# The S5 chunk recurrence: 64 sequential steps over pairs of chunks replaced by a tree with two more levels

## The chip, the core and the metric

The kernel runs on one NeuronCore of a Trainium2 chip, in one launch. The time is device microseconds of that core. Five engines run side by side and meet through semaphores: TensorE (PE, matrix products), VectorE (DVE), ScalarE (ACT), GpSimd (POOL) and SyncE (SP, which issues most of the DMAs).

## What is computed

Two trunk layers for 1024 latent tokens and 128 prompt ("context") tokens, with shared weights. Layer 0 feeds a differential attention and an S5 state-space mixer from one input projection; layer 1 is a pooling mixer; each layer ends in a squared-ReLU MLP. The change concerns the S5 mixer alone, whose core in the reference is

```python
bu = einsum(u, b_bar)                      # per token, 32 groups x 64 complex states, two directions
elems = (broadcast(a), bu)                 # h[t] = a * h[t-1] + bu[t], complex
_, _, h_re, h_im = lax.associative_scan(complex_affine_combine, elems, reverse=reverse, axis=1)
y = einsum(h_re, c_re) - einsum(h_im, c_im)
```

The state `h` at the end of the prompt's scan is an output too.

## The kernel before

**Layout of the scan.** The tokens are cut into chunks of C8 = 8. That leaves NCL = 128 chunks of the latent tokens and NCX = 16 of the prompt. A tile `ST` (128 partitions = two directions x 64 states) holds for real and imaginary part (2), for each of the G = 32 groups, SLOTS = 147 chunk states of 4 bytes each in a row: slots 0 to 128 are the latent's, from CX0 = 130 on the prompt's. Matrix products put each chunk's own contribution there; what is left is the recurrence over chunks, `state[c+1] += a^8 * state[c]`, a complex product and sum.

**The levels.** `carry(..., 1, ...)` first adds, for all pairs of chunks at once, the odd slot into the even one (level 0, on DVE and POOL, while the products land). Then `scan_step(j)`, j = 0 to 63, walks the even slots one after another with a^16 (`ar16`, `ai16`): four DVE instructions (`t1 = cur*ar`, `t2 = swapped cur*ai`, `t1 + t2`, `nxt + t1`), each over 2 x 32 = 64 elements per partition, and in the first eight steps over 128, since the prompt's chain is walked beside the latent's. Last, `carry(..., 2, ...)` fills in the odd slots, for two groups at a time. The two temporaries are the tiles `sc1`, `sc2`; the traces name all of them `sc`.

**Where the steps stand.** After the S5 inputs the kernel runs 36 *blocks*, n = 0 to 35: 12 weight tiles (query, key, value of four heads) times three column blocks of 384 tokens. A block takes 24 matrix products (`pmm`) on PE; DVE multiplies the sum by the row norm (`zz <- pmm,y` or `vz <- pmm,y` in `unscaled`), ACT adds a bias and, for queries and keys, copies the two halves crosswise, DVE multiplies by the cosines (`zz <- zz,cos`), POOL does the sine part, and the result is written out by SP while the next block runs (`finish`). In nearly the same blocks POOL builds 16 output tables of the S5 mixer (`in_ri`, `in_t`, six instructions each, `s5_table`; DVE the first of them), PE makes window products of them (`pk`) and the modulation vectors (`pm`). The scan steps are strewn over these blocks: `scan(SC(n)[0])` behind `zz <- pmm,y`, `scan(SC(n)[1])` after the middle of the block. `SC` gives none for n < 4 and two and two from then on, so 64 steps fill the blocks 4 to 19. The second `carry` follows from block 21 on, the output products from block 24.

**What sets the order.** From block 3 on (`i == 1`) all five engines are pinned to program order (`pinned.update(PIN)`), so each engine's queue runs as the code is written. The pmm sums have four buffers in PSUM, the `zz`/`vz` tiles three.

Of the kernel before, what the change touches and what calls it, by code (L numbers as in the profile page):

```python
# [8 lines left out]
F32 = mybir.dt.float32  # L9
# [3 lines left out]
ALU = mybir.AluOpType  # L13
# [14 lines left out]
G = 32  # L28
C8 = 8
NCL, NCX = TL // C8, TX // C8  # L30
CX0 = NCL + 2
# [6 lines left out]
EPS = 1e-6  # L38
RB = 3
CV = 5  # L40
SC = lambda n: (0, 0) if n < 4 else (2, 2)
PIN = "TPVSA"
PINA = "T"
L0 = (3,)
# [28 lines left out]
def build(nc, tc, a, o, probe=None):  # L73
    pinned = set()

    class Engine:
# [5 lines left out]
        def __getattr__(self, op):  # L82
            f = getattr(self.e, op)

            def call(*args, **kw):
                ins = f(*args, **kw)  # L86
                if self.name in pinned:
# [5 lines left out]
    V, A, T, P, S_ = (Engine(n, e) for n, e in (("V", nc.vector), ("A", nc.scalar), ("T", nc.tensor),  # L93
                                                ("P", nc.gpsimd), ("S", nc.sync)))
# [25 lines left out]
    def tt(e, out, x, y, op):  # L120
        return e.tensor_tensor(out, x, y, op=op)

    def stt(e, out, x, s, y, op0, op1):
        e.scalar_tensor_tensor(out, x, s, y, op0=op0, op1=op1)
# [53 lines left out]
    YB = [3]  # L178
    H = Pool("H", side="left")
    UR = Pool("u", side="left")  # L180
    ar8, ai8, ar16, ai16 = (UR([128, 2, G], F32, nm) for nm in ("ar8", "ai8", "ar16", "ai16"))

    def u_tile():
        return UR([128, C8, UC], F32, "U", bufs=4)
# [295 lines left out]
    pw = S([128, 2, 9, G], F32, "pw")  # L480
# [4 lines left out]
    def cmul(e, ore, oim, xr, xi, yr, yi, tmp, neg_im=False):  # L485
# [11 lines left out]
         b2(0, 2).to_broadcast([128, 2, G]), b2(1, 2).to_broadcast([128, 2, G]), ptmp[:, :2])  # L497
    cmul(V, pw[:, 0, 5:9], pw[:, 1, 5:9], pw[:, 0, 1:5], pw[:, 1, 1:5],
         b2(0, 4).to_broadcast([128, 4, G]), b2(1, 4).to_broadcast([128, 4, G]), ptmp)
    V.tensor_copy(ar8, pw[:, 0, 8:9].to_broadcast([128, 2, G]))  # L500
    V.tensor_scalar(ai8[:, 0], pw[:, 1, 8], -1.0, None, op0=ALU.mult)
    V.tensor_copy(ai8[:, 1], pw[:, 1, 8])
    tt(V, ar16, ar8, ar8, ALU.mult)
    tt(V, ai16, ai8, ai8, ALU.mult)
    tt(V, ar16, ar16, ai16, ALU.subtract)
    stt(V, ai16, ar8, 2.0, ai8, ALU.mult, ALU.mult)

    fden = S([128, 3, G], F32, "fden")
    tt(V, fden[:, 0], lre, lre, ALU.mult)
# [113 lines left out]
    ST = R([128, G, 2, SLOTS], F32, "ST").rearrange("p g r s -> p r g s")  # L623
# [14 lines left out]
    def proj_load(i):  # L638
        if i < 12:
            wq[i] = W([128, KT, 128], F32, "raw1")  # L640
            dma(wq[i], a["w_in"][4 + i])
# [12 lines left out]
    for gi, g0 in enumerate(range(0, G, 3)):  # L654
        n = min(3, G - g0)
# [19 lines left out]
    RP = Pool("rope", side="right")  # L675
# [53 lines left out]
    dma(sin, a["sin"])  # L729
    rp = lambda shape, dt, name: RP(shape, dt, name, bufs=3, tag="rp")  # L730

    def scan_step(j):
        sh = [128, 2, G]
        if j < NCX // 2:
            cur = ST[:, :, :, 2 * j:2 * j + CX0 + 1:CX0]
            nxt = ST[:, :, :, 2 * j + 2:2 * j + CX0 + 3:CX0]
            sh = sh + [2]
            ar, ai = ar16[:, :, :, None].to_broadcast(sh), ai16[:, :, :, None].to_broadcast(sh)
        else:
            cur, nxt, ar, ai = ST[:, :, :, 2 * j], ST[:, :, :, 2 * j + 2], ar16, ai16  # L740
        t1 = RP(sh, F32, "sc1")
        t2 = RP(sh, F32, "sc2")
        tt(V, t1, cur, ar, ALU.mult)
        tt(V, t2, cur[:, ::-1], ai, ALU.mult)
        tt(V, t1, t1, t2, ALU.add)
        tt(V, nxt, nxt, t1, ALU.add)

    pvt = Pool("pvt", side="right", space=PSUM)
    psn.close()
# [20 lines left out]

        finish(last)

    step = [0]

    def scan(n):
        for _ in range(n):
            if step[0] < NCL // 2:
                scan_step(step[0])
                step[0] += 1

    def unscaled(b, p, cf, z):

        tt(V, z, p, ys[b], ALU.mult)
        scan(SC(n)[0])
        for s0, s1, q in SEGS[b]:
            A.activation(z[:, s0:s1], z[:, s0:s1], AF.Identity, bias=cf[:, q:q + 1])

    def qk_block(h, kind, b, p, cf, mid):
# [9 lines left out]
        mid()  # L798
        scan(SC(n)[1])

# [20 lines left out]
    def v_block(h, b, p, cf, mid):  # L821
# [3 lines left out]
        mid()  # L825
        scan(SC(n)[1])

# [15 lines left out]
    def out_tiles(oc):  # L843

        if oc % 2 == 0:
            m = UR([128, BBN], F32, "mE", tag="bb")
            ori = S3([128, 2, 4, 128], F32, "ori", tag="craw")
            return (ori[:, 0], ori[:, 1]), m[:, :512].rearrange("p (g x) -> p g x", g=4), (
                UR([128, 2, 2, UC], F32, "E", tag="pout"), m[:, 512:].rearrange("p (r g c) -> p r g c", r=2, g=2))
        ori = [S3([128, 4, 128], F32, nm, tag="in_ri", bufs=2) for nm in ("orr", "oii")]  # L850
        return ori, S3([128, 4, 128], F32, "mt"), [W([128, 2, 2, UC], F32, "E", tag="raw", bufs=2) for _ in range(2)]

    def out_load(oc, ori, mt):
        g0 = 4 * oc
        for r, x in enumerate(ori):
            dma(x, oS[r, g0:g0 + 4].rearrange("g p m -> p g m"))
        dma(mt, mS[g0:g0 + 4].rearrange("g s h x -> (s h) g x"))
# [79 lines left out]
    def after(n):  # L937
        i, k = divmod(n, 3)
        for m in range(G // 2):
            if tab_at(m) == n:  # L940
                tabs[m] = s5_table(m)
                tabs[m][0]()
        oc = n - NS
        if 0 <= oc < 8:
            assert step[0] >= NCL // 2
            ori, mt, E = outs[oc] = out_tiles(oc)
            out_load(oc, ori, mt)

    def post(n):
        oc = n + 1 - NS  # L950
        if 0 <= oc < 8:
            assert step[0] >= NCL // 2
            for g2 in range(2):
                carry(V, 4 * oc + 2 * g2, 2, 2, *(RP([128, 2, 2, UC // 2], F32, nm) for nm in ("sc1", "sc2")))
        oc = n - NS
        if 0 <= oc < 8:
            for g2 in range(2):
                out_states(oc, g2, outs[oc][2][g2])
# [3 lines left out]
    n, loads = 0, None  # L962
    for i in range(12):
        h, kind = divmod(i, 3)
        if i == 1:
            pinned.update(PIN)
        proj_load(i + 1)
        w, cf = wq.pop(i), None
        for b in (2, 0, 1):
            p, last, *c = project(w, b)  # L970
            cf = c[0] if c else cf
            before(n)
            if n in KN:
                keys_in(KN[n])
            (qk_block if kind < 2 else v_block)(h, *((kind,) if kind < 2 else ()), b, p, cf, lambda: after(n))
            post(n)
            if b == 2:
                proj_split(i + 1)
            if n == NS + 9:
                S3.close()  # L980
                R.close()
                UR.close()
                HB = Pool("heads", side="right")
                KL = [[HB([128, KEYS + TX], F32R, f"Kl{j}{m}") for m in range(2)] for j in range(2)]
                for kl in KL:
                    for m in range(2):
                        P.memset(kl[m].bitcast(F32)[64 - 64 * m:128 - 64 * m], 0.0)
                loads = load_head(0)
            if loads:
                next(loads, None)  # L990
            n += 1
        if kind == 1 and h not in KH:
            keys_in(h)
        if step[0] == NCL // 2:
            step[0] += 1
            sfin = RP([128, 2, G], F32, "sfin")
            V.tensor_copy(sfin, ST[:, :, :, UC])
            dma(o["ns"], sfin)
# [23 lines left out]
    cur = {}  # L1022
# [291 lines left out]
    for b in range(NB):  # L1314
        t = BB([128, KT, BX], F32R, "blk", bufs=3)
        for k in range(4):
            src = hid([128, BN], F32, ("ph", "pl")[k % 2])
# [58 lines left out]
    t0, t1 = MODV[0]  # L1376
# [356 lines left out]
```

## Time and profile before

| | us |
|---|---|
| three runs, median (lowest to highest) | 2555.7 (2552.96 to 2557.45) |
| the profiled execution, its time | 2552.76 |
| its span, first to last instruction | 2551.0 |
| busy: PE / DVE / ACT / POOL | 2399.8 / 1792.0 / 877.2 / 267.0 |
| blocks 4 to 19, by the DVE's `pmm,y` rows | 178.0 to 312.0 |

Read the page by stage. Its line of forty slices (each 63.8 us) has PE at 9 tenths in nearly all of the span, but at 6 to 8 in most of the first eight slices, where DVE stands at 7 to 9. The shares over the whole span hide that; the views that follow are of the stretch 178 to 312 us.

### The profile page before, as it was taken

The page shows a single profiled execution, that of the slowest core. Times are in us where ns is not written, and L with a number is a line of the kernel's source. Part 1 is how long each engine was busy: PE and PEld are TensorE (multiplying, and loading weights), DVE is VectorE, ACT ScalarE, POOL GpSimd, SP SyncE. Part 2 cuts the span into 40 slices and gives each one's busy share as a digit, 9 for nine tenths or more (in the row PEclk, how much of TensorE's full clock was granted, in tenths as well). Part 3 has the DMA queues.
Part 4 walks back from the last instruction along what each step waited for, and adds up shares of the span by engine and source line. Part 5 has one row for each costly group of instructions (what it writes and reads, how often), then busy time and mean ns, then how long its engine had stood idle before and what let it go on. Part 6 is the DMA issues. An engine that isn't in the chain of part 4 may idle for free.

```text
span 2551.0 us, 36404 instructions
## 1 busy us (share of the span) xinstructions
PE 2399.8 (94%) x14070; PEld 2296.1 (90%) x14070; DVE 1792.0 (70%) x3583; ACT 877.2 (34%) x1663; POOL 267.0 (10%) x274
## 2 busy tenths in 40 slices
PE   7987898898997999999999999889999999999996
PEld 3876697787897999999999999879999999999996
DVE  7379865889788777767777655886565555555557
ACT  4453365777615221222222222562122222222214
POOL 5455612100000000000000000120000000000002
PEclk8998998999998999999999999989999999999998
DMA  6334688423353232322332110011111111111102
GB/s 244 82 104 126 192 200 229 105 57 81 129 191 108 67 91 68 98 75 75 91 91 79 50 34 25 1 50 50 42 50 34 50 34 50 34 50 42 42 9 74
DMA packets 106491, 210.86 MB, mean 83 GB/s; under 512 B 10576, under 2 KB 67664, under 8 KB 105936
## 3 DMA queue, kind: packets, MB, share of 16 engines
q1 hardware_dynamic: 104080, 203.01, 27.0%
q10 hardware_dynamic: 2240, 5.54, 0.6%
q8 instruction: 111, 1.82, 0.3%
q14 instruction: 60, 0.49, 0.1%
HBM read 176.95 MB, written 31.56 MB: 82 GB/s over the span
## 4 chain that ended last, share of the span: by engine, by line
PE 64%; DVE 11%; issue 5%; ACT 4%; DMA 4%; POOL 1%; SPq 0%; POOLq 0%; DVEq 0%; ACTq 0%
PE p L86 61%; DVE mj L86 2%; DVE blk L86 1%; DMA raw<-in_w_dram 1%; DVE sc L86 1%; DMA raw<-in_mod_v_dram 1%; PE SP L86 1%; DVE nm L86 1%; ACT e L86 1%; PE tp L86 1%; DVE x L86 1%; DVE s L86 1%; ACT blk L86 1%; DVE zz L86 1%; DVE w2l L86 1%
## 5 line engine op out<-in xcount | busy, mean ns | idle before, releaser
L86 PE MATMUL p<-blk,wh 128*128 128x384 f32 (+1 forms) x3072 | 794.2, 340 | 0.0
L86 DVE SCALAR_TENSOR_TENSOR x<-p,modc,x 128x384 f32<-128x384 f32 (+2 forms) x1056 | 513.6, 513 | 142.6 <-PE p L86 138.7
L86 PEld LDWEIGHTS p<-blk,wh 128*128 128x128 f32 x3072 | 561.5, 189 | 1.6 <-issue 1.2
L86 PE MATMUL p<-blk,wl 128*128 128x384 f32 (+1 forms) x1536 | 520.8, 339 | 0.0
L86 PE MATMUL p<-ph,w2h 128*128 128x384 f32 x1536 | 514.9, 335 | 3.7 <-DVE x L86 3.7
L86 PE MATMUL p<-pl,w2h 128*128 128x384 f32 x1536 | 513.9, 335 | 0.0
L86 PE MATMUL p<-ph,w2l 128*128 128x384 f32 x1536 | 513.6, 334 | 0.0
L86 ACT ACTIVATE r<-r,cf 128x384 f32<-128x384 f32 (+2 forms) x256 | 129.8, 531 | 691.6 <-DVE r L86 691.5
L86 PEld LDWEIGHTS p<-ph,w2h 128*128 128x128 f32 x1536 | 288.3, 188 | 6.2 <-DVE x L86 3.6
L86 PEld LDWEIGHTS p<-blk,wl 128*128 128x128 f32 x1536 | 289.5, 188 | 0.1
L86 PEld LDWEIGHTS p<-pl,w2h 128*128 128x128 f32 x1536 | 288.3, 188 | 0.3
L86 PEld LDWEIGHTS p<-ph,w2l 128*128 128x128 f32 x1536 | 288.3, 188 | 0.1
L86 DVE TENSOR_TENSOR r<-p,y 128x384 f32<-128x384 f32 x192 | 106.2, 554 | 188.9 <-PE p L86 188.7
L86 ACT ACTIVATE wh<-raw 128x1024 fp32r<-128x1024 f32 x80 | 84.7, 1060 | 349.7 <-PE p L86 312.1
L86 DVE SCALAR_TENSOR_TENSOR mj<-raw,cb 128x1024 f32<-128x1024 f32 x128 | 156.1, 1220 | 13.6 <-DMA raw<-in_mod_v_dram 12.6
L86 ACT ACTIVATE w2h<-raw 128x1024 fp32r<-128x1024 f32 x74 | 77.3, 1057 | 221.2 <-PE p L86 161.5
L86 PE MATMUL pmm<-lo,wh 128*128 128x384 f32 (+1 forms) x384 | 137.8, 359 | 7.8 <-DVE lo L86 7.5
L86 PE MATMUL pmm<-hi,wh 128*128 128x384 f32 (+1 forms) x384 | 141.0, 368 | 0.8 <-ACT wh L86 0.8
L86 PE MATMUL pmm<-hi,wl 128*128 128x384 f32 (+1 forms) x384 | 136.6, 356 | 1.2 <-DVE wl L86 1.2
L86 DVE TENSOR_TENSOR s<-r 128x384 f32<-128x384 f32 x192 | 106.5, 555 | 40.1 <-ACT r L86 40.0
L86 POOL TENSOR_TENSOR pl<-pl,mx 128x256 f32<-128x256 f32 x18 | 18.6, 1039 | 1024.1 <-ACT pl L86 1024.1
L86 DVE TENSOR_TENSOR wl<-raw,wh 128x1024 fp32r<-128x1024 f32 x76 | 98.7, 1300 | 22.1 <-ACT wh L86 21.8
(278 smaller groups left out, 3346.5 us busy)
## 6 DMA issues: line engine op xcount, KB each, us to landing
raw<-in_w_dram SPq DMA_DIRECT2D x128, 512.0 KB, 3.6
raw<-in_mod_v_dram SPq DMA_DIRECT2D x64, 512.0 KB, 3.6
raw<-in_mod_w_dram SPq DMA_DIRECT2D x25, 512.0 KB, 4.6
raw<-in_w_in_dram SPq DMA_DIRECT2D x16, 512.0 KB, 4.8
Kd<-kS SPq DMA_DIRECT2D x32, 176.0 KB, 4.8
qS<-zz SPq DMA_DIRECT2D x12, 384.0 KB, 2.7
Q<-qS SPq DMA_DIRECT2D x32, 144.0 KB, 4.7
x<-in_x_dram SPq DMA_DIRECT2D x3, 1536.0 KB, 7.3
```

Source lines behind the costliest of these rows:

```text
L86: ins = f(*args, **kw)
```

## The change

`scan_step` is replaced by a generator `scan_pieces`. Level 0 and its counterpart (`carry`) stay as they are. On the 64 even slots two more levels are put: level 1 joins slots 2 and 4 of each group of four chunks (multiplier a^16, 32 joins per group of states in the latent's row, so every fourth slot is read), level 2 joins slots 4 and 8 of each eight (a^32, 16 joins, every eighth slot). What is left is walked sequentially over every eighth slot with a^64: 16 steps. Then the two levels are walked back down to fill in the slots between. A level is cut into pieces of at most 256 elements: level 1 into eight pieces of four groups each (2 x 4 x 32) and one for the prompt (2 x 32 x 4), level 2 into four of eight groups (2 x 8 x 16) and one for the prompt (2 x 32 x 2). Up and down that is 2 x (9 + 5) = 28 pieces. A piece, as a step, is four DVE instructions. `SC` becomes one call behind `pmm,y` and two after the middle, so the 44 calls fill the blocks 4 to 18 (the last call, the 45th, ends the generator). The multipliers a^8, a^16, a^32 and a^64 are squared from one another in the prologue (four instructions each on 32 or 64 elements) and held without the doubled real part.

```diff
-SC = lambda n: (0, 0) if n < 4 else (2, 2)
+SC = lambda n: (0, 0) if n < 4 else (1, 2)
...
-    ar8, ai8, ar16, ai16 = (UR([128, 2, G], F32, nm) for nm in ("ar8", "ai8", "ar16", "ai16"))
+    pws8 = [(UR([128, 1, G], F32, f"ar{8 << i}"), UR([128, 2, G], F32, f"ai{8 << i}")) for i in range(4)]
...
-    V.tensor_copy(ar8, pw[:, 0, 8:9].to_broadcast([128, 2, G]))
+    ar8, ai8 = pws8[0]
+    V.tensor_copy(ar8[:, 0], pw[:, 0, 8])
     V.tensor_scalar(ai8[:, 0], pw[:, 1, 8], -1.0, None, op0=ALU.mult)
     V.tensor_copy(ai8[:, 1], pw[:, 1, 8])
-    tt(V, ar16, ar8, ar8, ALU.mult)
-    tt(V, ai16, ai8, ai8, ALU.mult)
-    tt(V, ar16, ar16, ai16, ALU.subtract)
-    stt(V, ai16, ar8, 2.0, ai8, ALU.mult, ALU.mult)
+    for (ar, ai), (ar2, ai2) in zip(pws8, pws8[1:]):
+        tt(V, ar2, ar, ar, ALU.mult)
+        tt(V, ai2[:, 0:1], ai[:, 0:1], ai[:, 0:1], ALU.mult)
+        tt(V, ar2, ar2, ai2[:, 0:1], ALU.subtract)
+        stt(V, ai2, ar.to_broadcast([128, 2, G]), 2.0, ai, ALU.mult, ALU.mult)
...
-    def scan_step(j):
-        sh = [128, 2, G]
-        if j < NCX // 2:
-            cur = ST[:, :, :, 2 * j:2 * j + CX0 + 1:CX0]
-            nxt = ST[:, :, :, 2 * j + 2:2 * j + CX0 + 3:CX0]
-            sh = sh + [2]
-            ar, ai = ar16[:, :, :, None].to_broadcast(sh), ai16[:, :, :, None].to_broadcast(sh)
-        else:
-            cur, nxt, ar, ai = ST[:, :, :, 2 * j], ST[:, :, :, 2 * j + 2], ar16, ai16
-        t1 = RP(sh, F32, "sc1")
-        t2 = RP(sh, F32, "sc2")
+    def advance(src, dst, lvl, g0, n, cnt, every):
+
+        cur = ST[:, :, g0:g0 + n, src:src + every * (cnt - 1) + 1:every]
+        nxt = ST[:, :, g0:g0 + n, dst:dst + every * (cnt - 1) + 1:every]
+        ar, ai = (t[:, :, g0:g0 + n, None].to_broadcast([128, 2, n, cnt]) for t in pws8[lvl])
+        t1 = RP([128, 2, n, cnt], F32, "sc1")
+        t2 = RP([128, 2, n, cnt], F32, "sc2")
         tt(V, t1, cur, ar, ALU.mult)
         tt(V, t2, cur[:, ::-1], ai, ALU.mult)
         tt(V, t1, t1, t2, ALU.add)
         tt(V, nxt, nxt, t1, ALU.add)
 
+    def scan_pieces():
+
+
+        def level(lvl, first, second):
+            span = 2 << lvl
+            cnt = NCL // span
+            n = min(G, 128 // cnt)
+            for g0 in range(0, G, n):
+                advance(first, second, lvl, g0, n, cnt, span)
+                yield
+            advance(CX0 + first, CX0 + second, lvl, 0, G, NCX // span, span)
+            yield
+
+        yield from level(1, 2, 4)
+        yield from level(2, 4, 8)
+        for j in range(NCL // 8):
+            if j < NCX // 8:
+                advance(8 * j, 8 * j + 8, 3, 0, G, 2, CX0)
+            else:
+                advance(8 * j, 8 * j + 8, 3, 0, G, 1, 1)
+            yield
+        yield from level(2, 0, 4)
+        yield from level(1, 0, 2)
...
     def scan(n):
         for _ in range(n):
-            if step[0] < NCL // 2:
-                scan_step(step[0])
-                step[0] += 1
+            if not scanned[0] and next(steps, 0) == 0:
+                scanned[0] = 1
```

On DVE, at the start of block 4 (a key block), the rows before are the first two steps and the cosine product behind them:

```order
L86 TENSOR_TENSOR zz<-pmm,y_386 128x384
L86 TENSOR_TENSOR sc_1654<-ST,ar_107 128x128
L86 TENSOR_TENSOR sc_1655<-ST,ai_108 128x128
L86 TENSOR_TENSOR sc_1654<-sc_1654,sc_1655 128x128
L86 TENSOR_TENSOR ST<-ST,sc_1654 128x2x32x2
L86 TENSOR_TENSOR sc_1660<-ST,ar_107 128x128
L86 TENSOR_TENSOR sc_1661<-ST,ai_108 128x128
L86 TENSOR_TENSOR sc_1660<-sc_1660,sc_1661 128x128
L86 TENSOR_TENSOR ST<-ST,sc_1660 128x2x32x2
L86 TENSOR_TENSOR zz<-zz,cos 128x384
```

The same place on DVE now:

```order
L86 TENSOR_TENSOR zz<-pmm,y_398 128x384
L86 TENSOR_TENSOR sc_1666<-ST,ar_107 128x256
L86 TENSOR_TENSOR sc_1667<-ST,ai_108 128x256
L86 TENSOR_TENSOR sc_1666<-sc_1666,sc_1667 128x256
L86 TENSOR_TENSOR ST<-ST,sc_1666 128x2x4x32
L86 TENSOR_TENSOR zz<-zz,cos 128x384
```

One piece of 256 elements stands where two steps of 128 stood; its last index (32) runs over every fourth slot of `ST`, where before the last index (2) ran from the latent's slot to the prompt's.

On DVE in block 10 (a query block, in the middle of the scan), before, from the norm product to the cosine product:

```order
L86 TENSOR_TENSOR zz<-pmm,y_386 128x384
L86 TENSOR_TENSOR sc_2156<-ST,ar_107 128x64
L86 TENSOR_TENSOR sc_2157<-ST,ai_108 128x64
L86 TENSOR_TENSOR sc_2156<-sc_2156,sc_2157 128x64
L86 TENSOR_TENSOR ST<-ST,sc_2156 128x2x32
L86 TENSOR_TENSOR sc_2162<-ST,ar_107 128x64
L86 TENSOR_TENSOR sc_2163<-ST,ai_108 128x64
L86 TENSOR_TENSOR sc_2162<-sc_2162,sc_2163 128x64
L86 TENSOR_TENSOR ST<-ST,sc_2162 128x2x32
L86 TENSOR_TENSOR zz<-zz,cos 128x384
```

And now:

```order
L86 TENSOR_TENSOR zz<-pmm,y_398 128x384
L86 TENSOR_TENSOR sc_2132<-ST,ar_111 128x64
L86 TENSOR_TENSOR sc_2133<-ST,ai_112 128x64
L86 TENSOR_TENSOR sc_2132<-sc_2132,sc_2133 128x64
L86 TENSOR_TENSOR ST<-ST,sc_2132 128x2x32
L86 TENSOR_TENSOR zz<-zz,cos 128x384
```

Here one step of 64 elements, one of the 16 sequential ones, stands between the two products instead of two.

## Rows read from the trace of the kernel before

**Rows 1.** Chain of waits in 258 to 312 us, shares of that stretch by line.

```profile
by line: DVE sc L86 32.1%; DVE zz L86 11.3%; DVE ST L86 8.4%; DMA raw<-in_mod_w_dram 7.7%; DMA vS<-vz 6.7%; issue 5.4%; DMA kS<-zz 5.1%; DVE wl L86 3.1%; PE pk L86 2.3%; SPq L86 2.2%; PE pm L86 1.9%; DVE vz L86 1.0%; DVE chl L86 0.8%; ACT k
```

**Rows 2.** Stretches: from:to, length, busy us (instructions) of each engine, granted clock.

```profile
core 0: us, PE busy (x) PEld busy (x) DVE busy (x) ACT busy (x) POOL busy (x), PEclk, DMA share, GB/s
178.00:220.50 42.50, 31.59 (x230) 28.54 (x229) 39.68 (x93) 11.41 (x27) 25.27 (x34) 0.88 0.44 117
220.50:264.10 43.60, 36.72 (x236) 29.36 (x235) 41.86 (x97) 15.95 (x34) 27.31 (x34) 0.85 0.36 102
264.10:312.00 47.90, 44.09 (x311) 34.79 (x309) 43.23 (x114) 15.69 (x35) 26.91 (x37) 0.99 0.67 198
```

**Rows 3.** The same view of the scan's instructions alone (tile sc, DVE).

```profile
178.00:312.00 134.00, 97.52 (x256) 0.91 0.49 141
```

**Rows 4.** DVE's timeline, an undisturbed 64-element step and the next one's start.

```profile
200.45 0.27 DVE L86 TENSOR_TENSOR sc<-ST,ar 128x64 f32<-128x64 f32 x1
...
200.92 0.23 DVE L86 TENSOR_TENSOR sc<-sc,sc 128x64 f32<-128x64 f32 x1
201.18 0.27 DVE L86 TENSOR_TENSOR ST<-ST,sc 128x64 f32<-128x64 f32 x1
201.49 0.27 DVE L86 TENSOR_TENSOR sc<-ST,ar 128x64 f32<-128x64 f32 x1
```

**Rows 5.** DVE's timeline, an undisturbed 128-element step and the next one's start.

```profile
191.05 0.39 DVE L86 TENSOR_TENSOR sc<-ST,ar 128x128 f32<-128x128 f32 x1
...
191.79 0.29 DVE L86 TENSOR_TENSOR sc<-sc,sc 128x128 f32<-128x128 f32 x1
192.11 0.41 DVE L86 TENSOR_TENSOR ST<-ST,sc 128x128 f32<-128x128 f32 x1
192.56 0.41 DVE L86 TENSOR_TENSOR sc<-ST,ar 128x128 f32<-128x128 f32 x1
```

**Rows 6.** DVE's timeline, an undisturbed `carry` of 292 elements, every second slot.

```profile
327.87 0.47 DVE L86 TENSOR_TENSOR sc<-ST,ar 128x292 f32<-128x292 f32 x1
...
328.74 0.46 DVE L86 TENSOR_TENSOR sc<-sc,sc 128x292 f32<-128x292 f32 x1
329.24 0.46 DVE L86 TENSOR_TENSOR ST<-ST,sc 128x292 f32<-128x292 f32 x1
```

**Rows 7.** DVE groups in 475 to 700 us: form, count, busy us, mean ns.

```profile
L86 DVE SCALAR_TENSOR_TENSOR blk<-uf,blk 128x256 fp32r<-128x256 f32 x3 | 1.9, 643 | 0.0
L86 DVE SCALAR_TENSOR_TENSOR blk<-uf,blk 128x128 fp32r<-128x128 f32 x3 | 1.2, 415 | 0.0
```

**Rows 8.** DVE's timeline, a 64-element step beside POOL's work, and the next step's start.

```profile
208.64 0.52 DVE L86 TENSOR_TENSOR sc<-ST,ar 128x64 f32<-128x64 f32 x1
...
210.65 0.52 DVE L86 TENSOR_TENSOR sc<-ST,ar 128x64 f32<-128x64 f32 x1
```

**Rows 9.** POOL's timeline in the same microseconds.

```profile
208.44 0.65 POOL L86 TENSOR_TENSOR in_t<-pout,craw 128x256 f32<-128x256 f32 x1
209.16 0.72 POOL L86 TENSOR_TENSOR in_ri<-in_ri,in_t 128x256 f32<-128x256 f32 x1
209.84 0.64 POOL L86 TENSOR_TENSOR in_ri<-pout,craw 128x256 f32<-128x256 f32 x1
210.44 0.64 POOL L86 TENSOR_TENSOR in_t<-pout,craw 128x256 f32<-128x256 f32 x1
```

**Rows 10.** DVE's timeline, block 20, which has no steps between its products.

```profile
312.00 0.55 DVE L86 TENSOR_TENSOR zz<-pmm,y 128x384 f32<-128x384 f32 x1
314.31 0.56 DVE L86 TENSOR_TENSOR zz<-zz,cos 128x384 f32<-128x384 f32 x1 [1.77 <-ACT zz L86]
```

**Rows 11.** DVE's timeline in the prologue: the squarings and what follows.

```profile
19.04 0.22 DVE L86 TENSOR_TENSOR ar<-ar,ai 128x64 f32<-128x64 f32 x1
19.17 0.69 DVE L86 TENSOR_TENSOR bb<-ff,in_ri 128x512 f32<-128x512 f32 x1
...
24.81 2.01 DVE L86 TENSOR_TENSOR wl<-raw,wh 128x1024 fp32r<-128x1024 f32 x1
26.75 11.46 DVE L86 SCALAR_TENSOR_TENSOR lo<-x,avec,hi 128x384 fp32r<-128x384 f32 x8
```

**Rows 12.** PE's timeline: its first wait for those.

```profile
28.42 0.44 PE L86 MATMUL pmm<-lo,wh 128*128 128x384 f32 x1 [3.89 <-DVE lo L86]
```

More of the change, by code (lines that the diff above doesn't have):

```diff
@@ L771, in keys_in @@
         finish(last)
-    step = [0]
+    steps, scanned = scan_pieces(), [0]
     def scan(n):
         for _ in range(n):
-            if step[0] < NCL // 2:
-                scan_step(step[0])
-                step[0] += 1
+            if not scanned[0] and next(steps, 0) == 0:
+                scanned[0] = 1
     def unscaled(b, p, cf, z):
@@ L944, in after @@
         if 0 <= oc < 8:
-            assert step[0] >= NCL // 2
+            assert scanned[0]
             ori, mt, E = outs[oc] = out_tiles(oc)
@@ L951, in post @@
         if 0 <= oc < 8:
-            assert step[0] >= NCL // 2
+            assert scanned[0]
             for g2 in range(2):
@@ L993, in build @@
             keys_in(h)
-        if step[0] == NCL // 2:
-            step[0] += 1
+        if scanned[0] == 1:
+            scanned[0] = 2
             sfin = RP([128, 2, G], F32, "sfin")
```

## The prediction

> **What bounds the kernel now.** The page's share of busy time says PE, and for most of the span that is so. The scan does not live there: it lives in blocks 4 to 19, 178 to 312 us, so I read that stretch by itself. First its busy times, in three parts [rows 2]: DVE is busy 39.7 of 42.5, 41.9 of 43.6 and 43.2 of 47.9 us, together 124.8 of 134.0; PE 31.6, 36.7 and 44.1, together 112.4. So DVE is the full engine here, by a wide margin in the first part, by a small one in the second, and level with PE in the third. Then the scan's own share [rows 3]: 256 instructions, 97.5 us, nearly three quarters of the stretch. Then the chain of waits for its last part [rows 1]: the scan's rows (sc and ST) are 40.5% of what released the end, the other rope products of DVE 12%, and the DMAs in it are issued behind a DVE result. So what DVE spends on the scan in this stretch is paid in time, nearly one for one, until PE takes over.
>
> **What a step costs now.** Undisturbed, a 64-element step runs from 200.45 to 201.49, 1.04 us [rows 4], and a 128-element step from 191.05 to 192.56, 1.51 us [rows 5]. 56 of the one and 8 of the other are 58.2 + 12.1 = 70.3 us. The scan really takes more. Its 97.5 us are busy time; after three of the four instructions of a step there is a gap of about 0.03 us (200.92 + 0.23 to 201.18 [rows 4]), 64 x 0.09 = 5.8 us, so it holds DVE for 103.3 us. The other 33.0 us are a meeting with POOL: beside POOL's table work the same step takes from 208.64 to 210.65, 2.01 us [rows 8], while POOL completes three instructions (starts 208.44 to 210.44) [rows 9]. That is 0.97 us more for three, 0.32 us for each POOL instruction. POOL runs 34 + 34 + 37 = 105 instructions in the stretch [rows 2], and 33.0 / 105 is 0.31, so one price for each POOL instruction accounts for all of it.
>
> **What a piece of 256 elements costs.** No row shows that shape, so I bound it. The lower end is the `carry`, which reads every second slot, 8 bytes apart: 292 elements from 327.87 to 329.24 + 0.46 and a gap, 1.86 us [rows 6]; 36 elements fewer, at the 1.0 ns an element that the contiguous sum shows (0.23 to 0.29 us for 64 more [rows 4, 5]), four times, are 0.15 less: 1.71 us. The upper end comes from the 128-element step. There the instructions that touch `ST` grow from 0.27 to 0.41 us for 64 elements more, 2.2 ns an element, twice the contiguous sum's [rows 4, 5]: reading far apart (the two elements of a row are 520 bytes apart) costs double. 128 elements more are then 3 x 0.28 + 0.13 = 0.97 on top of 1.51: 2.48 us. Which end holds for slots 16 bytes apart (level 1) and 32 bytes apart (level 2)? For 32 bytes there is a row: the split of the GELU result writes and reads every eighth element, and it takes 415 ns for 128 elements and 643 for 256, 1.8 ns an element [rows 7]; with that slope a piece is 1.51 + 3 x 0.23 + 0.13 = 2.33. For 16 bytes there is none. I take double cost there too, since every element of a 16-byte stride is as alone as at 32 bytes, and 2.4 us for a piece, between 2.33 and 2.48.
>
> [...]
>
> **The change, term by term.**
> 1. Pieces and steps, undisturbed. A sweep is 9 + 4 pieces at 2.4 and one of 128 elements at 1.51: 32.7 us, two sweeps 65.4. The sequential part is 2 steps at 1.51 and 14 at 1.04: 17.6. Together 83.0 against 70.3: **+12.7 us**. The instructions fall from 256 to 176, but the elements that each of the four goes over in all rise from 56 x 64 + 8 x 128 = 4608 to 26 x 256 + 4 x 128 + 14 x 64 = 8064, most of them at double price.
> 2. The meeting with POOL. The number of POOL instructions is the same, and by the count above the price goes by them: 0. Bounds: if it is paid for each DVE instruction, 33.0 / 256 = 0.129 each and 80 fewer, -10.3; if it grows with the time that the scan holds DVE, 33.0 x 12.7 / 70.3 = +6.0. I take 0, because 64- and 128-element instructions both fit the price for each POOL instruction.
> 3. The cover of ACT's latency. `zz <- zz,cos` can start 2.31 us after `zz <- pmm,y` starts, when ACT is free [rows 10]. Two steps of 1.04 behind 0.48 of the product filled that; one step does not (1.52), and DVE would wait 0.8 us. This concerns blocks 9 to 13 (queries and keys that have one sequential step there); a piece of 2.4 covers it, and so does one step beside POOL (0.48 + 2.01). Between 0 and 5 x 0.8 = 4; I take **+2**. Queued behind that wait on DVE is the rest of the block's scan, and nobody but DVE's own next block waits for it.
> 4. Block 19 has no scan any more. Its old steps are in the 103.3, so that gain is inside term 1.
> 5. The multipliers. Eight more small instructions in the prologue, 0.13 us each from start to start between others (19.04 to 19.17), 0.22 alone [rows 11]: 1.0 to 1.8. DVE has no gap there down to the first `lo`, for which PE waits 3.89 us [rows 12], so it is paid: **+1.2**.
> 6. What PE takes back. In the third part PE is busy 44.1 of 47.9 [rows 2], so a longer DVE there is not paid in full where PE would have been late anyway; and PE may use up to four finished sums as a store. Between 0 and -4; I take **-2**.
>
> The sum is 12.7 + 0 + 2 + 1.2 - 2 = +13.9 us. The profiled execution took 2552.76 us (span 2551.0 and 1.8 around it), so it would become 2566.7. That execution is as fast as the fastest of the three runs; on their median of 2555.7 the sum gives **2569.6 us**, 0.54% slower.
>
> **The rivals.**
> *An instruction is the price, faster.* If a DVE instruction here costs a fixed time, the meeting with POOL included, plus 1.0 ns an element wherever the elements lie, fewer and longer instructions win. The place is the 28 pieces: 26 x (1.71 - 2.4) = -17.9 on term 1 makes it -5.2, and term 2 goes to -10.3. With the 2 of term 3 and 1.2 of term 5: -12.3, 2543.4 us. It decides from the piece's price: the 28 pieces may take 103.3 less the sequential part (17.6 and its share of POOL, about 8), 77.7 us, 2.8 us each with POOL's part; below that the change gains, and my forecast has 65.4 + 25, 3.2 each. For it speaks the `carry` at 1.0 ns an element [rows 6]; against it the doubled slope of 128 elements and of the 32-byte rows [rows 5, 7].
> [...]
> *Half of it, no difference.* Either level 1 reads at full rate (18 x 0.69 = -12.4 on term 1) or the meeting with POOL is paid for each instruction (-10.3), not both: +1.5 to +3.6, about 2558 us. For the first speaks that no row shows 16 bytes; for the second that the 64-element rows beside POOL are stretched one by one.
> *More than the sum, slower.* Longer instructions hold POOL up, POOL holds DVE up in turn for as long as the scan lasts (+6.0), the cover of term 3 fails in full (+2 more) and PE gives nothing back (+2): +24, 2579.5 us. POOL's 79.5 busy us of 134 [rows 2] leave it room, which speaks against it.
> That the change does not do what it says I leave out: the new order shows 176 instructions of the shapes named.
>
> **How the numbers follow.** What this kernel's measurement can tell from no change is about 0.2%, 5 us: 2550.6 to 2560.8. The forecast (2562 to 2575) has a chance of 0.55, the worse case 0.13; both are slower, 0.68. Half of it is 0.17 and counts as the same. The instruction as the price is 0.15, faster. The range leaves out the faster rival and little else: from 2551 (the half case with a little more) to 2581.
>
> **What would show each step.** In the changed kernel's groups, `sc <- ST,ar` of 256 elements at a minimum of 0.65 to 0.70 us says double cost, 0.42 to 0.45 says full rate; level 1 (2x4x32) and level 2 (2x8x16) can be told apart by their place, blocks 4 to 6 and 7. The scan's busy time in its stretch should be some 110 us for 176 instructions; near 90 the faster rival holds. Block 19 should start at about 312 + 6 us or later, though it is the first without scan. A wait of `zz <- zz,cos` for ACT should stand in blocks 9 to 13, up to 0.8 us each. POOL's instructions should number the same and be some tenths longer beside a piece. The prediction is wrong if the 256-element instructions read at full rate, or if the stretch grows and later stages close the gap: PE then would show fewer waits between 312 and 420 us.

## The result, and the profile after

The changed kernel takes 2566.4 us (median of four runs, 2563.5 to 2568.1) against 2554.3 (2552.9 to 2557.5), slower by 12.0 us. The recorded ratio is 1.0053 with a 95% interval of 1.0041 to 1.0065, which would be 13.5 us; beside the later experiments the kernel before had medians of 2552.0 to 2553.2, and against those it is 13.2 to 14.4. So the loss is 12 to 14 us; where a difference to after is taken below, it is taken from 12.0. Forecast were 2569.6 us and slower. The sign and nearly the size are right, but four of the six terms that make up the sum are off by amounts that happen to cancel.

The profiled execution of after took 2566.43 us, its span is 2563.9 (2551.0 before). Three starting points of a block say where the 12.9 us of span lie. Block 4, the first with scan, starts 4.4 us late (182.4 for 178.0). Block 20 starts 16.0 us late (328.0 for 312.0), so blocks 4 to 19 take 145.6 us instead of 134.0, +11.6. At the end 12.9 are left: 3.1 are given back behind the scan.

The same three stretches as [rows 2], by blocks, and the scan's instructions alone as in [rows 3]; the columns are those of before (length; busy us and count of PE, PEld, DVE, ACT, POOL; granted clock; DMA share; GB/s):

```profile
182.40:232.30 49.90, 36.51 (x249) 33.24 (x248) 48.59 (x73) 11.43 (x28) 30.41 (x34) 0.83 0.38 103
232.30:275.00 42.70, 33.61 (x217) 25.90 (x216) 37.02 (x78) 15.96 (x34) 27.62 (x33) 0.83 0.35 101
275.00:328.00 53.00, 46.52 (x299) 36.11 (x298) 48.05 (x73) 15.89 (x35) 28.58 (x32) 0.88 0.63 179
...
182.40:328.00 145.60, 105.49 (x176) 0.85 0.46 130
```

DVE's instructions in the three stretches fall from 304 to 224 and its busy time rises from 124.8 to 133.7 us. The scan's own went from 97.5 us for 256 to 105.5 for 176. The first and the last stretch, where the pieces of 256 elements stand, became longer; the middle one, of single steps, holds DVE for less and still takes 42.7 us, which is a wait, shown further down. The granted clock is lower than before in each (0.83, 0.83 and 0.88 for 0.88, 0.85 and 0.99); PE stands idle for 29.0 us here instead of 21.6, and the chain names DVE.

The chain of waits for the last part (270 to 328 us), in the columns of [rows 1]:

```profile
by line: DVE sc L86 35.9%; DVE ST L86 11.3%; DVE zz L86 10.2%; DMA raw<-in_mod_w_dram 6.9%; DMA kS<-zz 4.7%; issue 4.7%; PE pk L86 3.6%; PE pm L86 3.3%; DVE wl L86 3.0%; ACT zz L86 2.9%; DVE vz L86 1.9%; PE pvt L86 1.5%; DVE chl L86 0.7%; S
```

The scan's share (sc and ST) is 47%, from 40.5%: DVE sets the end of this stretch still, and a little more so.

DVE's timeline of after, an undisturbed piece on the way down (level 1, every fourth slot) with the start of the next (start, duration):

```profile
297.52 0.60 DVE L86 TENSOR_TENSOR sc<-ST,ar 128x256 f32<-128x256 f32 x1
298.03 0.61 DVE L86 TENSOR_TENSOR sc<-ST,ai 128x256 f32<-128x256 f32 x1
298.68 0.42 DVE L86 TENSOR_TENSOR sc<-sc,sc 128x256 f32<-128x256 f32 x1
299.14 0.61 DVE L86 TENSOR_TENSOR ST<-ST,sc 128x256 f32<-128x256 f32 x1
299.78 0.60 DVE L86 TENSOR_TENSOR sc<-ST,ar 128x256 f32<-128x256 f32 x1
```

A piece takes 2.26 us. The three instructions that touch `ST` take 0.60 or 0.61 each, the sum of the two temporaries, which lie in a row, 0.42. A level-2 piece, every eighth slot, shows the same duration in block 7:

```profile
216.34 0.60 DVE L86 TENSOR_TENSOR sc<-ST,ar 128x256 f32<-128x256 f32 x1
```

So slots 16 and 32 bytes apart cost the same (0.60), and both cost more than the 292 elements at 8 bytes of [rows 6] (0.47).

The waits of the cosine product, first all of them in 182.4 to 328.0, from the groups of DVE (count; busy us, mean ns; idle before):

```profile
L86 DVE TENSOR_TENSOR zz<-zz,cos 128x384 f32<-128x384 f32 x10 | 7.6, 756 | 6.2 <-ACT zz L86 6.2
```

and then the one in block 12, in DVE's timeline:

```profile
256.62 0.55 DVE L86 TENSOR_TENSOR zz<-pmm,y 128x384 f32<-128x384 f32 x1
257.09 0.28 DVE L86 TENSOR_TENSOR sc<-ST,ar 128x64 f32<-128x64 f32 x1
...
257.83 0.27 DVE L86 TENSOR_TENSOR ST<-ST,sc 128x64 f32<-128x64 f32 x1
259.12 0.56 DVE L86 TENSOR_TENSOR zz<-zz,cos 128x384 f32<-128x384 f32 x1 [1.02 <-ACT zz L86]
```

One step stands between the two products, and DVE then idles 1.02 us until ACT has written `zz`. In blocks 9 to 13 these waits are 0.56, 0.82, 0.86, 1.02 and 1.12 us, 4.4 together, and 1.77 more in block 19, which has no scan any more.

The prologue, on DVE (the last two instructions of the new squarings, between other work):

```profile
24.54 1.08 DVE L86 TENSOR_TENSOR ar<-ar,ai 128x32 f32<-128x32 f32 x1
25.65 1.27 DVE L86 COPY pout<-pw 64x512 f32<-64x512 f32 x1
26.96 2.18 DVE L86 TENSOR_TENSOR wl<-raw,wh 128x1024 fp32r<-128x1024 f32 x1
29.06 1.12 DVE L86 SCALAR_TENSOR_TENSOR ai<-ar,ai 128x64 f32<-128x64 f32 x1
30.11 1.47 DVE L86 SCALAR_TENSOR_TENSOR lo<-x,avec,hi 128x384 fp32r<-128x384 f32 x1
```

on POOL, beside them,

```profile
24.29 1.28 POOL L86 TENSOR_TENSOR in_t<-pin,bb 128x512 f32<-128x512 f32 x1
...
28.02 2.09 POOL L86 TENSOR_TENSOR in_ri<-pin,bb 128x512 f32<-128x512 f32 x1
```

and on PE, whose wait for `lo` answers to [rows 12]:

```profile
31.63 0.69 PE L86 MATMUL pmm<-lo,wh 128*128 128x384 f32 x1 [7.09 <-DVE lo L86]
```

These two instructions, of 32 and 64 elements, took 1.08 and 1.12 us while POOL worked on 512 elements. The first `lo` is 3.4 us later than in [rows 11] and PE's wait 3.2 us longer.

### The profile page after: what moved, and what is told of

The parts are those of the page before. It is cut to its first block, busy times and chain, and to the rows that moved or that the text cites. A ratio compares the mean times of both kernels' runs of the same rounds, so it can differ in the third digit from the quotient of the medians.

```text
span 2563.9 us, 36332 instructions
## 1 busy us (share of the span) xinstructions
PE 2405.3 (94%) x14070; PEld 2299.1 (90%) x14070; DVE 1803.2 (70%) x3511; ACT 877.4 (34%) x1663; POOL 278.4 (11%) x274
## 4 chain that ended last, share of the span: by engine, by line
PE 65%; DVE 11%; issue 5%; ACT 4%; DMA 3%; POOL 1%; SPq 0%; POOLq 0%; DVEq 0%; ACTq 0%
PE p L86 62%; DVE mj L86 2%; DVE sc L86 1%; DVE blk L86 1%; PE SP L86 1%; DVE nm L86 1%; ACT e L86 1%; DMA raw<-in_w_dram 1%; PE tp L86 1%; DVE x L86 1%; DMA raw<-in_mod_v_dram 1%; DVE zz L86 1%; DVE s L86 1%; ACT blk L86 1%; ACT zz L86 1%
## 5 line engine op out<-in xcount | busy, mean ns | idle before, releaser
L86 DVE SCALAR_TENSOR_TENSOR mj<-raw,cb 128x1024 f32<-128x1024 f32 x128 | 156.1, 1220 | 12.7 <-DMA raw<-in_mod_v_dram 11.6
L86 POOL TENSOR_TENSOR pl<-pl,mx 128x256 f32<-128x256 f32 x18 | 18.6, 1037 | 1024.8 <-DVE yr L86 1010.6
L86 DVE TENSOR_TENSOR wl<-raw,wh 128x1024 fp32r<-128x1024 f32 x76 | 99.6, 1311 | 21.6 <-ACT wh L86 21.5
```

## The experiments

The kernel before ran again beside each group; every difference is to it.

**1. The prologue by itself.** The twelve squarings of after, with the 64 old steps on every second slot.

```diff
+        for j in range(NCL // 2):
+            if j < NCX // 2:
+                advance(2 * j, 2 * j + 2, 1, 0, G, 2, CX0)
+            else:
+                advance(2 * j, 2 * j + 2, 1, 0, G, 1, 1)
+            yield
```

> The 64 old steps (two and two a block), with the changed kernel's multipliers (a^8 to a^64 squared from one another in the prologue); the last two pairs are computed and not used. Theory: the multipliers are dearer than I had said, because the last two squarings came to stand beside POOL's tables and took about 1.1 us each; in the changed kernel the first lo was 3.2 us later and block 4 began 4.4 us later, and all of that is theirs: +3.5 to +4.4 us, about 2558.5 against 2554.3. Rival (my term): eight instructions of 0.13 to 0.22 us, +1.0 to +1.8, about 2555.5, and the later start of block 4 comes from elsewhere.

2556.4 us against 2553.2, ratio 1.0014 (1.0005 to 1.0023): +3.3. Block 4 starts at 180.7 (+2.7), the scan's stretch takes 135.1 (+1.1). DVE's timeline shows the two long squarings again:

```profile
23.90 1.09 DVE L86 TENSOR_TENSOR ar<-ar,ai 128x32 f32<-128x32 f32 x1
...
28.42 1.12 DVE L86 SCALAR_TENSOR_TENSOR ai<-ar,ai 128x64 f32<-128x64 f32 x1
```

So the multipliers cost some 3 us and not 1.2: the price is the meeting with POOL (1.09 and 1.12 us here, beside products of 512 elements; 0.22 in [rows 11]), not the instruction. The same old steps come out differently here too: their 256 instructions are busy for 100.5 us in the stretch, 3.0 more than in [rows 3], beside as many POOL instructions. That is how far two traces of the same work can lie apart.

**2. The squarings moved out of the prologue,** to block 3, behind the point where the engines are pinned.

```diff
             pinned.update(PIN)
+            for (ar, ai), (ar2, ai2) in zip(pws8, pws8[1:]):
+                tt(V, ar2, ar, ar, ALU.mult)
...
```

> The changed kernel with all twelve squarings moved from the prologue to the start of block 3, where DVE waits for ACT. Theory: block 4 begins 4 to 5 us earlier than in the changed kernel, less at most 1.5 us for the squarings themselves: 2562 to 2563 us. Rival: the time lost in the prologue is given back to PE later, or the squarings cost as much in block 3: 2565 to 2567.

2565.1 against 2553.2, 1.0048 (1.0036 to 1.0061): +12.0, nothing won. Block 0 does start at 156.2, 3.1 us earlier than in after, but blocks 2 and 3 give it back: the way from block 2 to block 3 takes 17.3 us instead of 14.7, and the squarings stand there in DVE's queue from 171.19 to 175.57, again with POOL beside the first of them:

```profile
171.19 0.99 DVE L86 TENSOR_TENSOR ar<-ar 128x32 f32<-128x32 f32 x1
172.10 0.77 DVE L86 TENSOR_TENSOR ai<-ai 128x32 f32<-128x32 f32 x1
```

The rival held: the cost moved along. In after DVE has 1.73 us of idle time ahead of block 3's norm product, waiting for a DMA:

```profile
176.13 0.56 DVE L86 TENSOR_TENSOR zz<-pmm,y 128x384 f32<-128x384 f32 x1 [1.73 <-DMA qS<-zz]
```

The squarings, 4.4 us with POOL beside them, filled that and made the way 2.6 us longer. The wait for ACT that they were meant to fill (1.95 us in block 3) comes behind the norm product, and it is still there.

**3. The cover of ACT's latency.** Two calls behind `pmm,y` and one after the middle.

```diff
-SC = lambda n: (0, 0) if n < 4 else (1, 2)
+SC = lambda n: (0, 0) if n < 4 else (2, 1)
```

> The changed kernel with two calls behind the norm product and one after the middle of a block (SC = 2, 1). Theory: the waits of zz <- zz,cos for ACT in blocks 9 to 13 (0.56 to 1.12 us, 4.4 in all) vanish, and the time falls by 3 to 4.4 us: about 2562.5. Rival: DVE's idle time let POOL work undisturbed and comes back as contention, so that the waits go and the time stays: 2565.5 to 2566.5.

2561.1 against 2553.2, 1.0033 (1.0021 to 1.0044): +7.9, so 4 us less than after (5 by the two medians). The group of cosine products in the scan's stretch has only block 19's wait left, and the stretch takes 138.9 us instead of 145.6:

```profile
L86 DVE TENSOR_TENSOR zz<-zz,cos 128x384 f32<-128x384 f32 x10 | 6.7, 673 | 1.8 <-ACT zz L86 1.8
```

That is the mechanism of term 3, and at least twice its size.

**4. The distance of the slots.** The pieces of the two levels go over every second slot (8 bytes), with the same instructions and the same number of elements. These are the wrong slots, so its states are not the reference's.

```diff
+        every = min(every, 2) if lvl < 3 else every
         cur = ST[:, :, g0:g0 + n, src:src + every * (cnt - 1) + 1:every]
```

> The changed kernel with the 28 pieces of levels 1 and 2 on slots 8 bytes apart instead of 16 and 32: as many instructions of as many elements, but wrong slots, so the states are not the reference's. Theory: a piece costs 1.71 us undisturbed instead of 2.26, 26 x 0.55 = 14.3 us less on DVE in a stretch that DVE bounds, 11 to 14 us in the end: 2552 to 2555. Rival (the price is the instruction, or the length, not the distance): the groups of 256 elements stay at 0.60 us and the time at 2566.

2553.8 against 2553.2, 1.0005 (0.9996 to 1.0014): +0.6. The scan's instructions in the stretch, and the sum into `ST` among DVE's groups:

```profile
180.90:314.00 133.10, 93.98 (x176) 0.90 0.50 142
```

```profile
L86 DVE TENSOR_TENSOR sc<-sc,sc 128x256 f32<-128x256 f32 x26 | 15.3, 588 | 0.9
L86 DVE TENSOR_TENSOR ST<-ST,sc 128x256 f32<-128x256 f32 x26 | 14.9, 574 | 0.9
L86 DVE TENSOR_TENSOR sc<-ST,ar 128x256 f32<-128x256 f32 x26 | 14.5, 559 | 0.4
```

The same groups of after:

```profile
L86 DVE TENSOR_TENSOR ST<-ST,sc 128x256 f32<-128x256 f32 x26 | 21.2, 816 | 0.9
L86 DVE TENSOR_TENSOR sc<-ST,ar 128x256 f32<-128x256 f32 x26 | 17.4, 671 | 0.4
L86 DVE TENSOR_TENSOR sc<-sc,sc 128x256 f32<-128x256 f32 x26 | 14.9, 572 | 0.9
```

At 8 bytes the sum into `ST` is as short as the sum of temporaries; in after it takes 816 ns instead of 574, and the sum of temporaries, which reads no slots, has hardly changed. These means hold POOL's part; undisturbed, a piece of experiment 4 takes 1.59 us and each of its instructions what the sum of temporaries takes:

```profile
199.91 0.42 DVE L86 TENSOR_TENSOR sc<-ST,ar 128x256 f32<-128x256 f32 x1
...
201.16 0.43 DVE L86 TENSOR_TENSOR ST<-ST,sc 128x256 f32<-128x256 f32 x1
201.50 0.42 DVE L86 TENSOR_TENSOR chl<-chl 128x256 fp32r<-128x256 f32 x1
```

The distance alone is worth 11.5 us of the scan's busy time and 11.4 us of the kernel's, about as much as the change loses in all. It isn't that the old steps read close elements: from group to group theirs lie 2 x 147 x 4 = 1176 bytes apart, and they pay too (0.27 us against 0.23 for the sum of temporaries [rows 4]). The tree pays for more of them, 8064 against 4608 for each of the four instructions. For 256 elements the runs show two prices: 0.42 us at 8 bytes, 0.60 at 16 and at 32.

**5 and 6. What the meeting with POOL is paid by.** In before, and then in after, POOL's six products of a table become six fills, which read nothing. Both kernels get the same edit.

```diff
             e = V if i in TABV else P
+            if e is P:
+                for x in (xr, tmp, xr, xi, tmp, xi):
+                    P.memset(x, 0.0)
+                return
```

> The kernel before, with POOL's six table products per table replaced by six fills of the same tiles (they write and read nothing), so the S5 output tables are zero. Theory (the meeting costs DVE 0.31 us for each POOL instruction that reads): the scan's hold on DVE falls from 103.3 us by 84 x 0.31 = 26 to about 77, the 20 rope products of POOL keeping theirs. Rival (DVE's 64-element instructions are slow of themselves in this stretch): the hold stays above 95. The time falls by less than 26, since PE has 112 us of work in the stretch of 134: 2535 to 2545 us.

Before with fills: 2528.7 against 2552.3, 0.9909 (0.9892 to 0.9926), -23.6 us. The scan's instructions, and POOL's fills, 309 ns each:

```profile
178.20:292.60 114.40, 76.98 (x256) 0.93 0.58 166
```

```profile
L86 POOL MEMSET in_ri<- 128x256 f32 x54 | 16.0, 309 | 35.8 <-DMA oS<-in_ri 35.1 <-PE pm L86 0.7
```

With the gaps of 5.8 the scan holds DVE for 82.8 us instead of 103.3 [rows 3]: 20.5 less for 84 products of tables, 0.24 us each. Expected were 77 us, and 2535 to 2545 for the kernel.

> The changed kernel with the same fills for POOL's table products. Theory (price for each POOL instruction): the hold falls from 109.2 by 78 x 0.31 = 24 us to about 85. Rival (price for each DVE instruction, 26 / 256 = 0.10): by 176 x 0.10 = 18 to about 91. By the theory the tree stays 8 to 9 us dearer than the steps with POOL out of the way, by the rival it would be 14.

After with fills: 2543.1 against 2552.3, 0.9971 (0.9957 to 0.9985).

```profile
179.30:303.80 124.50, 86.76 (x176) 0.90 0.53 152
```

With its gaps of 3.7 us the scan holds DVE for 90.5 us instead of 109.2: 18.7 less for 78 products (one table's work lies outside the stretch), 0.24 each. The price for each POOL instruction is the same with 256 and with 176 DVE instructions; for each DVE instruction it is not (0.080 and 0.106). The hold of 90.5 us is near the 91 that the rival had been given, but only because its price was set from 26 us: with the 20.5 that experiment 5 measured the rival gives 109.2 - 176 x 0.080 = 95. So term 2 was rightly not given a gain for 80 fewer instructions. The tree without this meeting holds DVE 7.7 us longer than the steps, near the 9 of the undisturbed sum.

The timelines of the two engines, laid side by side, show the same row by row. In experiment 5 the scan's 56 instructions that run beside a fill alone take 0.1 us more in all than undisturbed ones; here is one, and the fill:

```profile
185.24 0.39 DVE L86 TENSOR_TENSOR sc<-ST,ai 128x128 f32<-128x128 f32 x1
185.14 0.31 POOL L86 MEMSET in_ri<- 128x256 f32 x1
```

In before, 89 that run beside a table product take 21.2 us more. One thing differs from the prediction: 0.31 was an average. The table products cost 0.24, and what is left (82.8 - 70.3 = 12.5 us) falls on the instructions beside POOL's 20 rope products of 384 elements, about 0.6 for each product. So the two runs set POOL's products against fills that read nothing: 0.24 us for each product, and 0.1 us in all for the 56 instructions beside a fill. A fill is also shorter (0.31 us against 0.64 to 0.72 in [rows 9]); that it is the reading alone was not shown.

**7 and 8. Another order in `ST`.** The groups go innermost, so that a piece and a step read neighbours: first in after (with the calls of experiment 3), then in before.

```diff
-    ST = R([128, G, 2, SLOTS], F32, "ST").rearrange("p g r s -> p r g s")
+    ST = R([128, SLOTS, 2, G], F32, "ST").rearrange("p s r g -> p r g s")
```

> The changed kernel with the state tile laid out slot by slot (the 32 groups of a slot side by side), the group as the innermost index of every carry and piece, and two calls before and one after the middle (SC = 2, 1). Everything is computed. Theory (the distance of the slots is the price): a piece reads runs of 4, 8 or 32 elements and costs about 1.7 us, a sequential step about 0.9, together 62 us instead of 79, and the cover is worth 5 more: 2545 to 2550 us, if ACT's writes and reads of the state tile, now 256 bytes apart, cost nothing on the path; with them dearer up to 2560. Rival (the price is the instruction's length): pieces stay at 2.26 and the time at the 2561 of the cover alone.

2568.2 against 2552.3, 1.0062 (1.005 to 1.0075): +15.9. The scan's busy time falls by 13.9 us against experiment 3 (undisturbed, 17 were expected), and its stretch

```profile
197.80:325.50 127.70, 90.40 (x176) 0.89 0.53 148
```

is 11 us shorter. But block 4 starts at 197.8, and the kernel is slower than all that was expected (2545 to 2561). ACT writes `ST` ahead of the blocks; its group there in 120 to 180 us, with elements of a row now 256 bytes apart,

```profile
L86 ACT ACTIVATE ST<-pin 64x438 f32<-64x438 f32 (+5 forms) x66 | 40.2, 673 | 4.3 <-PE pin L86 3.6
```

and the same group in before, with neighbours:

```profile
L86 ACT ACTIVATE ST<-pin 64x438 f32<-64x438 f32 (+5 forms) x66 | 24.1, 397 | 4.8 <-PE pin L86 4.0
```

16.1 us more on ACT, and nothing hides it there: PE waits 13.5 us for these writes, where before it waits 0.7, and block 4 is 16.9 us later than in experiment 3.

> The kernel before with the same layout of the state tile and the same order of indices. Everything is computed. Theory: a 64-element step, whose elements also lie far apart now, falls from 1.04 to 0.90 us and a 128-element one from 1.51 to 1.25: 56 x 0.14 + 8 x 0.26 = 10 us less on DVE, 2544 to 2548 us, faster than the kernel before, less what ACT's strided access costs. Rival: small steps gain nothing from it and ACT's cost shows: 2554 or more.

2570.9 against 2552.3, 1.0071 (1.0059 to 1.0082): +18.6, with block 4 at 195.3 and a stretch of 131.7. An undisturbed 64-element step takes 0.92 us instead of the 1.04 of [rows 4] (215.97 to 216.89). The scan's busy time is 93.2 (256 instructions), 4.3 less where I expected 10, and the kernel, expected at 2544 to 2548, is slower, with ACT's price in it. Most of a short instruction is not its elements (0.23 us for 64 close ones, 0.29 for 128 [rows 4, 5]), and what lies above the undisturbed sum stays: with the gaps of 5.8 the scan holds DVE for 99.0 us, 38 more than 56 x 0.92 + 8 x 1.17 = 60.9 (207.87 to 209.04 is a 128-element step), where before has 33.0. In the old steps there was little to win by order; in the pieces there was.

**9. Distance and cover together,** the edits of experiments 3 and 4.

> Both prices of the tree taken away at once: the pieces on slots 8 bytes apart (wrong slots, so the states are not the reference's) and two calls before, one after the middle of a block (SC = 2, 1). Theory (the two are independent and DVE still bounds the stretch): the 12.5 us of the distance and the 5 to 6 of the cover add up, 2554 - 5 = about 2548.5, 4 to 5 us faster than the kernel before, and blocks 4 to 19 take about 128 us. Rival (PE, with 112 us of work, takes over the stretch): the cover gives less than 2 us now, 2552 to 2553.

2548.2 against 2552.0, 0.9987 (0.9978 to 0.9996): -3.9, with a stretch of 126.9. Two causes, of some 12 and 4 us, add up, and without both the tree would be a little faster than the steps. No kernel that computes the reference got there. For that the slots would have to lie close from the first write on, and in experiment 7, where they do, ACT's writes cost more (block 4 is 16.9 us later) than DVE gains (a stretch 11.2 us shorter). A second, close copy of the even slots, written by the first `carry`, wasn't tried.

**10. One level less.** Level 1 up, 32 sequential steps with a^32, level 1 down, with the calls of experiment 3.

```diff
-        yield from level(2, 4, 8)
-        for j in range(NCL // 8):
-            if j < NCX // 8:
-                advance(8 * j, 8 * j + 8, 3, 0, G, 2, CX0)
+        for j in range(NCL // 4):
+            if j < NCX // 4:
+                advance(4 * j, 4 * j + 4, 2, 0, G, 2, CX0)
...
-        yield from level(2, 0, 4)
```

> The tree with one more level instead of two: level 1 up and down (18 pieces), 32 sequential steps with a^32 between, SC = 2, 1. Everything is computed; 200 DVE instructions instead of 176, but 6400 element positions for each of the four instead of 8064. Theory (distant elements are the price): undisturbed 18 x 2.26 + 4 x 1.51 + 28 x 1.04 = 75.8 us against 79.4, so 3 to 4 us less than the two-level tree with the same cover (2561): 2557 to 2558. Rival (an instruction is the price): 24 instructions more, 2563 or more.

2555.8 against 2552.0, 1.0016 (1.0007 to 1.0025): +3.8, of which some 3 are the prologue's, and about 4 us less than experiment 3, as the theory had it. But its mechanism is not what the trace shows. Blocks 4 to 19 take 134.6 us with 192 of the 200 instructions; the last two pieces stand in block 20. From block 4 to the end of block 20 the scan's instructions, here and then in experiment 3, are

```profile
181.10:323.80 142.70, 106.57 (x200) 0.89 0.50 143
```

```profile
180.90:325.69 144.79, 104.34 (x176) 0.88 0.49 141
```

busy for 2.2 us more, where the undisturbed sum has 3.6 less. What falls away instead is waiting: in experiment 3 the cosine products of blocks 19 and 20 wait 1.78 and 1.77 us for ACT, and here, where pieces stand in both blocks, neither does. The rows of block 20, experiment 3 first:

```profile
322.06 0.56 DVE L86 TENSOR_TENSOR zz<-zz,cos 128x384 f32<-128x384 f32 x1 [1.77 <-ACT zz L86]
```

```profile
321.94 0.55 DVE L86 TENSOR_TENSOR zz<-zz,cos 128x384 f32<-128x384 f32 x1
```

So 24 instructions more need not cost time, and that is all that this run decides. The price of far elements is shown by experiment 4.

## Why the prediction was right, and where its terms were not

What bounds the kernel, as the prediction has it, held: a longer DVE between blocks 4 and 19 was paid nearly one for one. The scan's hold grew by 5.9 us (109.2, that is 105.5 and gaps of 3.7, against 103.3) and the cosine product's waits by 6.2; together 12.1, and the stretch grew by 11.6. The sum came out near the measurement by luck: its errors have both signs.

The sizes that follow are each read from one trace.

*Term 1, the pieces, +12.7: too high by 3.6.* A piece takes 2.26 us where I took 2.4 between 2.33 and 2.48, so the sum is 26 x 2.26 + 4 x 1.51 + 14 x 1.04 = 79.4 against 70.3, +9.1. That a 16-byte distance costs as much as 32, which the prediction took without a row for it, was right (0.60 us each), and experiment 4 shows that the distance sets the price of a piece. The mis-sized step was the slope, 2.2 or 1.8 ns an element from the 128-element step and the split of the GELU result [rows 5, 7]; from 0.41 us at 128 elements to 0.60 at 256 it is 1.5, and the lower bound of the strided case lay above the measured piece.

*Term 2, POOL, 0: too high by 3.2.* The contention is 109.2 - 79.4 = 29.8 us for 98 POOL instructions in the stretch, 0.30 each, against 33.0 for 104, 0.32 (the prediction's 105 counts one twice that spans two of its three parts). The law held (experiments 5 and 6). About 2 us went with one table's six instructions, which fell outside the stretch; the rest is less than the 3.0 us by which experiment 1's trace differs from before with the same steps.

*Term 3, the cover, +2: too low by 2.4, and by 1.8 more in block 19.* The mechanism and the blocks were right, and so was the size of the single wait: in blocks 10 and 11 the way from product to product is 2.32 and 2.31 us, as in [rows 10], and the waits are 0.82 and 0.86. The step that failed was to take half of 5 x 0.8: every one of the five waits came, 4.4 us, just past the upper end. In blocks 9 and 12 ACT adds the bias in two pieces (0.80 us), since their column block holds prompt tokens too, where in block 20 of before it adds it in one (0.61), and the way becomes 2.50 us (block 12, then block 20 of before):

```profile
257.20 0.80 ACT L86 ACTIVATE zz<-zz,pcf 128x256 f32<-128x256 f32 x2 [3.68 <-DVE zz L86]
```

```profile
312.58 0.61 ACT L86 ACTIVATE zz<-zz,pcf 128x384 f32<-128x384 f32 x1 [4.98 <-DVE zz L86]
```

In block 13 ACT is busy with another tile (`kt`) until 266.32 and the way is 3.30 us, so DVE waits 1.12 although its step is longer beside POOL (0.61 us for each of its last two instructions, 0.22 and 0.27 in the step before). Block 19, which the text had gained inside term 1, has the same wait of 1.77 as block 20 of before; I priced its steps and not the cover that they had been. Experiment 3 takes back 4 us of the kernel's time by this alone.

*Term 5, the multipliers, +1.2: too low by 2 or more.* Experiment 1 measures 3.3 us of time, 2.7 at block 4. The step that failed was to take the price of small instructions from a place where POOL rests [rows 11]; these met POOL's products of 512 elements and took 1.08 and 1.12 us each. The same law as in term 2 stood in the prediction and was not applied here. In the profile of after block 4 is 4.4 us late. The 1.7 above experiment 1's are nearly absent in the kernels of experiments 3 and 4 too, which have the same prologue (0.2), and 0.6 of them stands ahead of the long squarings already (24.54 against 23.90); their cause stays open.

*Term 6, PE gives back, -2:* 1.4 us were given back from block 20 to block 35 (107.7 us for 109.1), where PE stands idle for 9.0 us instead of 11.1. Another 1.7 come after block 35, but there the twelve traces, with the same code, take anything from 2125.5 to 2132.1 us, so those can't be put down to the change.

Together 9.1 - 3.2 + 6.2 + 4.4 - 3.1 = 13.4, against 12.9 of span: terms 1 and 2 were 6.8 too high, 3 and 5 together 7.4 too low. The rival "an instruction is the price" falls with the piece of 2.26 us and with experiment 4; what was right in it is the piece at 8 bytes.

## What to carry to other kernels

Before instructions are merged into fewer, longer ones, count the elements that they go over and ask how far apart these lie: 80 DVE instructions fewer were worth less than 75% more elements at 16 and 32 bytes' distance, and worth more than the same elements at 8 (the scan is busy for 105.5 us with the ones, 94.0 with the others, and 97.5 in the old steps). An instruction that stands between a producer's hand-over and its use covers a latency (here 0.56 to 1.12 us in blocks 9 to 13 and 1.77 in block 19); when it is thinned out, count the cover of each such place, the emptied ones too. And a tiny instruction has the price of its place: beside POOL's products of 512 elements the two squarings took 1.08 and 1.12 us instead of 0.22. Moving the squarings to block 3 won nothing, since only 1.7 of their 4.4 us found DVE idle there.

## What the runs showed of the hardware

- On DVE, the scan's `f32` tensor-tensor instructions of 256 elements took 0.42 us from neighbouring elements and 0.60 at 16 and at 32 bytes' distance; at 8 bytes they took 0.42 too (experiment 4). No distance between 8 and 16 bytes was run, and 32 cost no more than 16.
- ACT's writes of `ST` were dearer too: with elements 256 bytes apart (experiment 7) an instruction took 673 ns in the mean, and 397 in a row.
- POOL's products of 256 elements cost DVE's scan 0.24 us each, whether DVE ran 256 or 176 instructions beside them (experiments 5 and 6); POOL's fills of the same tiles cost it 0.1 us for 56 instructions. Filled instead of computed they free 23.6 us of the old kernel, about 1%: more than either form of the scan is worth against the other.
